# Decoder layer on one core: forming the differences of x ahead of the weight splits, and moving the second pair's raw weights in the queues

## The chip, the cores and the metric

One core of one Trainium2 chip. The metric is the device time of one execution in microseconds; the time before is the median of 3 runs, 643.26 us (642.44 to 646.47).

## The reference

One layer of a post-norm decoder, batch 1, 512 tokens, width 1024, all in float32:

```python
proj = h @ w_in[l]                               # (512, 1024) @ (1024, 4096)
q, k, v, p, g = jnp.split(proj, [512, 1024, 1536, 2048], axis=-1)
y_attn = moba_attention(q.reshape(hs), k.reshape(hs), v.reshape(hs), rel_bias) @ w_branch_attn[l]
y_pool = multiscale_pool(p, w_pool_group[l], pool_scale[l]) @ w_branch_pool[l]
gates = jax.nn.sigmoid(g.astype(jnp.float32)).astype(h.dtype).reshape(B, S, N_BRANCHES, D)
mixed = gates[:, :, 0] * y_attn + gates[:, :, 1] * y_pool
h = layer_norm(ALPHA * h + mixed @ w_out[l], ln1_g[l], ln1_b[l])
a, u = jnp.split(h @ w_ffn_in[l], 2, axis=-1)    # 2 x 2816 columns
a = causal_dwconv(a, conv_w[l], conv_b[l])
f = (jax.nn.gelu(a, approximate=False) * u) @ w_ffn_out[l]
h = layer_norm(ALPHA * h + f, ln2_g[l], ln2_b[l])
```

The attention has 8 heads of 64 with a relative bias by distance; the pool mixer takes trailing means over 2, 4, 8 and 16 tokens for four groups of 128 channels. The change concerns the first tenth of the program, where `x @ w_in` is computed.

## The kernel before, in words

**Split products.** Every float32 matrix product is made of three matmuls (`mm3`). Each operand is split into a high half, a rounded copy that ACT makes, and a low half, the source minus that copy, which DVE makes (`split`, L70 and L71). The three matmuls are high by high, high by low and low by high.

**Chunks of weights.** `chunks` lists all weights in the order of use. `fetch` takes the next one: a DMA on SP's queue into `wraw` (three places), then the split into `whi` and `wlo` (five places, `RING`). `weights(i)` fetches up to three chunks ahead, but not beyond `state["limit"]`. Chunks 0 to 3 are the columns of v, chunk 4 is `p3` and chunk 5 is `p2` (two column tiles of the pool input, computed plainly by `in_tile`), chunks 6 to 9 are pair 0, chunks 10 to 13 pair 1, and so on up to pair 4.

**Pairs.** Two column tiles a and u are computed together by seven half-size products instead of eight (`seven`). Pair 0 holds pool tiles 0 and 1; pairs 1 to 4 hold one tile of q and one of k each. The weights of a pair come as four quarters: A (tile a as it is), X (u's first half twice, to which a's first half and u's second half are added), D (u's second half) and Y (made by DVE from X and A, L185). X needs two DMAs: a plain one on SP (L173), and, when that has landed, an accumulating one on POOL's queue (L175). A pair runs on PE in the order A twice, the Y part left over from the pair before, X, Y, D, X again, and keeps its last Y part for the next pair.

On the side of x, a pair needs four differences of the four blocks of x: nT1, T3, nT2, T4 (`t_form`, L244 and L247 on DVE), each split into halves. They are formed in place, in the two raw tiles `xr[0]` (blocks b11 and b12) and `xr[1]` (b21 and b22): nT1 and T3 replace `xr[0]`, nT2 and T4 replace `xr[1]`. Once they have been split, both tiles serve as places for raw weights (`homes`): X of pair n lies in one half of `xr[0]`, D of pair n in a quarter of `xr[1]`, and the two last quarters of `xr[1]` are working space of the pairs.

**The order around the change.** `load_x` brings x in eight tiles and splits each, with the four chunks of v between them. Then follow in the program: the split of the group weights `wg` (L350), the matmuls of v, during which `weights` fetches chunks 4 to 6 (p3, p2 and A of pair 0), the four differences with their splits (L475 to L478), the bias table `F_sb` (17 small copies, L372), `in_tile` for p3, its pool sum (four additions on DVE, L439), `write_end`, which fills the tile `neg` and writes it as the end of the strip table `F_d` in DRAM (L382 and L383), and `in_tile` for p2. The instructions of an engine are put in order when the program is built, by a planner that works with modelled times; the queues then run in that order. `tc.issue_after(ins)` holds the instructions of a block that lie on the engine of `ins` behind it on that engine, and leaves the other engines alone. `fetch` uses it to keep the plain DMA of pair 1's X behind the write of `neg` on SP:

```python
if (n, f, q) == ("i", 1, "X"):
    held.enter_context(tc.issue_after(state["neg"].ins))
```

`EARLY` and `AHEAD` say how many chunks ahead of its use a raw quarter is asked for. The first table of a strip is written by POOL (`write_table`, L378) behind the last accumulating DMA.

Of the kernel before, what the change touches and what calls it, by code (L numbers as in the profile page):

```python
# [10 lines left out]
AF = mybir.ActivationFunctionType  # L11
# [5 lines left out]
D = 1024  # L17
# [29 lines left out]
def layer_kernel(ctx: ExitStack, tc: tile.TileContext, xT, x, w_v, w_c, rel_bias, invcnt, w_group,  # L47
                 pscale, w_br, w_out, lnr, w_fi, convp, w_fo, out):
    nc = tc.nc
# [9 lines left out]
    def bank(name):  # L59
        return ps.tile([P, S], F32, tag="ps", name=name)  # L60
# [5 lines left out]
    def split(hi, lo, src, copy=None):  # L66
        if copy:
            copy(hi, src)
        else:
            nc.scalar.activation(hi, src, AF.Copy)  # L70
        state["lo"] = nc.vector.tensor_tensor(lo, src, hi.bitcast(F32), op=ALU.subtract)  # L71
        return state["lo"]

# [4 lines left out]
    at = {}  # L78
# [36 lines left out]
    state = {"next": 0, "limit": WO0 - 1}  # L115

    def fetch(pool=None, early=None):
        i = state["next"]
        state["next"] = i + 1
        for q, ahead in AHEAD.items():  # L120
            while coming[q]:
                key = coming[q][0]
                n, f = key
                lead_ = EARLY.get((n, f, q), ahead)
                if not homes.get((n, q)) or at[n, f, q] > i + (lead_ if q != "A" or (n, f - 1) in pair_of else 0):
                    break
                with ExitStack() as held:
                    if (n, f, q) == ("i", 1, "X"):
                        held.enter_context(tc.issue_after(state["neg"].ins))
                    if (n, f, q) in (("i", 1, "D"), ("i", 2, "A"), ("i", 2, "X"), ("i", 2, "D")):  # L130
                        held.enter_context(tc.issue_after(state["plain"].ins))
                    if (n, f, q) == ("i", 2, "X"):
                        held.enter_context(tc.issue_after(state["sum"].ins))
                    fetch_raw(coming[q].pop(0), q)
        if isinstance(chunks[i], tuple):
            ready[i] = (fetch_fo if i >= FO0 else fetch_seven)(i, *chunks[i])
            return
        raw = wp.tile([P, D], F32, tag="wraw", name=f"wraw{i}", bufs=3)
        if pool is None:
            hi = wp.tile([P, D], F32R, tag="whi", name=f"whi{i}", bufs=RING)  # L140
            lo = wp.tile([P, D], F32R, tag="wlo", name=f"wlo{i}", bufs=RING)
        else:
            hi = pool.tile([P, D], F32R, name=f"whi{i}")
            lo = pool.tile([P, D], F32R, name=f"wlo{i}")
        parts = 2 if early else 1
        for c in range(parts):
            sl = slice(c * (D // parts), (c + 1) * (D // parts))
            (nc.scalar if early else nc.sync).dma_start(raw[:, sl], chunks[i][:, sl])
            split(hi[:, sl], lo[:, sl], raw[:, sl], fast if early and c == 0 else None)
            if c == 0 and early:  # L150
                early()
        ready[i] = (hi, lo)
# [8 lines left out]
    homes = {(n, "A"): araw for n in "igf"}  # L161

    def fetch_raw(key, q):
        a, u = pair_of[key]
        r = raws[key, q] = homes[key[0], q](key[1])
        if q == "A":
            nc.sync.dma_start(r, a)
        elif q == "D":
            nc.sync.dma_start(r, u[:, S:])
        else:  # L170
            v = r.rearrange("p (a c) -> p a c", a=2)
            (pst, pn), (est, _) = u.ap
            state["plain"] = nc.sync.dma_start(  # L173
                v, bass.AP(tensor=u.tensor, offset=u.offset, ap=[[pst, pn], [0, 2], [est, S]]))
            state["acc"] = nc.gpsimd.dma_start(  # L175
                v, bass.AP(tensor=a.tensor, offset=a.offset, ap=[[pst, pn], [u.offset + S - a.offset, 2], [est, S]]),
                accum_op=ALU.add)
# [54 lines left out]
    t1, t2 = slice(0, 256), slice(256, 512)  # L232
    k1, k2 = slice(0, 4), slice(4, 8)
    parts = ("nT1", "T3", "nT2", "T4")
# [3 lines left out]
            pending.pop()()  # L238


    def t_form(n, tt, b11, b12, b21, b22):
        if n in ("nT1", "T3"):
            v, a = {"nT1": (b11, b11), "T3": (b12, b22)}[n]
            nc.vector.tensor_tensor(v, a, b12, op=ALU.subtract)  # L244
        else:
            v, a = {"nT2": (b22, b11), "T4": (b21, b22)}[n]
            nc.vector.scalar_tensor_tensor(v, a, -1.0, v, op0=ALU.mult, op1=ALU.subtract)  # L247
        split(*tt[n], v)

    def s_mm(key, q, part, act_, b, start, pin=False):  # L250
        wh, wl = split3(weights(at[(*key, q)]), 4 if q == "D" else KT)
# [48 lines left out]
    wg_raw = av.tile([P, 4, P], F32, tag="strip", name="wg_raw")  # L300
# [5 lines left out]
    ti = {n: tuple(pw.tile([P, 4, 256], F32R, name=f"i{n}_{q}") for q in ("hi", "lo")) for n in parts}  # L306
    pw.tile([P, 48], F32, name="pw_gap2")
    xr = [pw.tile([P, 4, S], F32, name=f"xr{n}") for n in range(2)]
# [38 lines left out]
                            compare_op=ALU.is_equal, fill=0.0)  # L347
    nc.sync.dma_start(wg_raw, w_group)
    wg_hi, wg_lo = (pb.tile([P, 4, P], F32R, name=f"wg_{q}") for q in ("hi", "lo"))
    split(wg_hi, wg_lo, wg_raw)  # L350

    behind.close()
    F_d = dram.tile([H, STRIP], F32, name="F_d")
# [6 lines left out]
    def make_table():  # L360
        F_sb = av.tile([P, S], F32, tag="strip", name="F_sb")
        (pst, pn), _ = rel.ap
        runs, lo_ = _bucket_runs(), 0
        while runs:
            b, n = runs.pop(0)
            step = 0
            if n == 1:
                while runs and runs[0] == [b + n, 1]:
                    step, n = -1, n + 1
                    runs.pop(0)  # L370
            at_ = rel.offset + b - step * (n - 1)
            nc.vector.tensor_copy(F_sb[:H, S - lo_ - n:S - lo_],  # L372
                                  bass.AP(tensor=rel.tensor, offset=at_, ap=[[pst, pn], [step, n]]))
            lo_ += n
        return F_sb
# [4 lines left out]
    def write_end():  # L380
        neg = av.tile([P, S], F32, tag="strip", name="neg")
        nc.vector.memset(neg[:H, :STRIP - S], NEG)  # L382
        state["neg"] = nc.sync.dma_start(F_d[:, S:], neg[:H, :STRIP - S])  # L383

    vv = av.tile([P, NT, H * DH], F32, name="vv", bufs=1)
    bs = [bank(f"v{j}") for j in range(NT)]
    for kt in range(KT):
# [41 lines left out]
    def pool_sum(j, b, sign=1.0, eng=None):  # L429
        eng = eng or nc.gpsimd  # L430
        w = POOL_WINDOWS[j]
        pt = pb.tile([P, PAD + S], F32, tag="tmp", name=f"pt{j}", bufs=TMP)
        nc.gpsimd.memset(pt[:, :PAD], 0.0)
        state["pt"] = nc.scalar.activation(pt[:, PAD:], b, AF.Copy, scale=sign)
        cur, sh = pt, 1
        while sh < w:
            nxt = pb.tile([P, PAD + S], F32, tag="tmp", name=f"pw{j}_{sh}", bufs=TMP)
            o = 2 * sh - 1
            state["sum"] = eng.tensor_tensor(nxt[:, o:], cur[:, o:], cur[:, o - sh:PAD + S - sh], op=ALU.add)  # L439
            cur, sh = nxt, 2 * sh  # L440
        sums[j] = pt, cur
# [22 lines left out]
    def in_tile(kind, j):  # L464
# [6 lines left out]
        else:  # L471
            gslot[j] = gates[:, len(gslot), :]
            nc.vector.tensor_copy(gslot[j], b)

    with tc.issue_after(state["xlo"].ins):  # L475
        t_form(parts[0], ti, xr[0][:, :, t1], xr[0][:, :, t2], xr[1][:, :, t1], xr[1][:, :, t2])
    for n in parts[1:]:
        t_form(n, ti, xr[0][:, :, t1], xr[0][:, :, t2], xr[1][:, :, t1], xr[1][:, :, t2])  # L478
    with tc.issue_after(state["lo"].ins):
        table = make_table()  # L480
    homes["i", "X"] = lambda n: xr[0][:, n % 2 * 2:n % 2 * 2 + 2, :].rearrange("p a c -> p (a c)")
    homes["i", "D"] = lambda n: xr[1][:, n % 2, :]
    raw_q = {}
    raw_k = {}
    state["limit"] = at["i", 0, "A"]
    pool_sum(PLAIN[0], in_tile("p", PLAIN[0]), eng=nc.vector)
    state["limit"] = WO0 - 1
    behind_sum = ExitStack()
    behind_sum.enter_context(tc.issue_after(state["sum"].ins))
    behind_sum.enter_context(tc.issue_after(state["pt"].ins))  # L490
    write_end()
    second = in_tile("p", PLAIN[1])

    def heads_done(p, ba):
# [166 lines left out]
    for f in range(KT - 1):  # L661
# [4 lines left out]
        for br in (1, 0):  # L666
            b = br_mm(f, br)
            if f < GSEVEN:
                t = gslot[8 * br + f]
                nc.vector.tensor_tensor(t, t, b, op=ALU.mult)  # L670
            else:
                t = branch[f, br] = unused.pop(0)
# [199 lines left out]
    def rd(c):  # L872
# [7 lines left out]
    tt = {n: tuple(sp.tile([P, 4, 256], F32R, name=f"{n}_{q}") for q in ("hi", "lo"))  # L880
          for n in ("nT1", "T3", "nT2", "T4")}
# [150 lines left out]
    cut = [bank(f"fo_cut{c}") for c in range(2)]  # L1032
# [23 lines left out]
def _bucket_runs():  # L1056
    b = _bucket_of_dist()
    runs = []
    for v in b:
        if runs and runs[-1][0] == v:  # L1060
            runs[-1][1] += 1
        else:
            runs.append([int(v), 1])
    return runs
# [53 lines left out]
```

## Time and profile before

| | before |
|---|---|
| median of 3 runs | 643.26 us (642.44 to 646.47) |
| the profiled execution | 642.5 us, its span 640.7 us |
| granted TensorE clock | 0.995 |
| PE busy | 627.9 us (98%) |
| DVE busy | 497.3 us (78%) |
| ACT busy | 348.7 us (54%) |
| POOL busy | 117.8 us (18%) |
| DMA | 106.11 MB, mean 166 GB/s |

The span runs from the first to the last instruction; the execution's own time is 1.8 us longer. PE is TensorE, DVE VectorE, ACT ScalarE, POOL GpSimd, SP SyncE, and SPq the DMA queue of SP. A row of the timeline gives the start, the duration, engine, line, operation, output and inputs, how many instructions it merges, and in brackets the idle time before it and what ended it. A row of the waits gives who waited for whom, the total in us, how often, and the longest. The tiles of the pairs of the input stage are called `sai`, `sbi` and `sci` on the output side; `iT` and `inT` are the split differences, `xT` the split x, `araw` the raw A and Y, and `xr` the raw X and D as well as the raw x.

### The profile page before, as it was taken

The numbers are of one execution on the slowest core, as the hardware profiler recorded it, in microseconds if no ns is written. First come the engines' busy times: TensorE is split into PE (matmuls) and PEld (weight loads), VectorE is DVE, ScalarE is ACT, GpSimd is POOL, SyncE is SP. The second block draws the span as 40 slices with busy tenths as digits, with TensorE's granted clock in tenths as the row PEclk, the third lists the DMA queues.
The fourth block names the chain that finished last, engine by engine and source line by source line (L and its number), as shares of the span: only waits on it lengthen the run. The fifth ranks groups of instructions, "written<-read, shape, count | busy, mean of one in ns | idle before, by whom it ended". The sixth has DMA issues, their size and how long they took to land.

```text
span 640.7 us, 10190 instructions
## 1 busy us (share of the span) xinstructions
PE 627.9 (98%) x3910; PEld 560.2 (87%) x3910; DVE 497.3 (78%) x755; ACT 348.7 (54%) x522; POOL 117.8 (18%) x129
## 2 busy tenths in 40 slices
PE   8999999999999999999999999999999999999994
PEld 6888998777788998889999999999998888888884
DVE  6977887786395787399776889888889649798696
ACT  6635777655544557225544566556666336555352
POOL 0032334233132111110010101011002102123202
PEclk9999999999999999999999999999999999999998
DMA  8387746522447515714086686877628955899905
GB/s 326 125 216 190 186 119 209 149 70 95 148 126 209 144 55 177 285 44 165 1 238 156 164 201 158 210 172 202 147 99 283 264 176 123 195 200 196 272 1 131
DMA packets 39312, 106.11 MB, mean 166 GB/s; under 512 B 4304, under 2 KB 4568, under 8 KB 39008
## 3 DMA queue, kind: packets, MB, share of 16 engines
q1 hardware_dynamic: 26576, 71.37, 33.2%
q0 software_dynamic: 12112, 33.05, 26.2%
q10 hardware_dynamic: 576, 1.05, 0.4%
q8 instruction: 30, 0.49, 0.3%
q14 instruction: 18, 0.15, 0.1%
HBM read 100.20 MB, written 3.17 MB: 161 GB/s over the span
## 4 chain that ended last, share of the span: by engine, by line
PE 94%; DMA 3%; DVE 2%; ACT 0%; issue 0%; DVEq 0%; SPq 0%; ACTq 0%
PE fi L226 5%; PE fi L227 5%; PE fi L223 5%; PE saf L223 4%; PE saf L227 4%; PE saf L226 4%; PE v L399 3%; PE g L223 2%; PE br L223 2%; PE g L227 2%; PE g L226 2%; PE br L226 2%; PE wo L223 2%; PE wo L226 2%; PE wo L227 2%; PE br L227 2%
## 5 line engine op out<-in xcount | busy, mean ns | idle before, releaser
L70 ACT ACTIVATE whi<-wraw 128x1024 fp32r<-128x1024 f32 (+1 forms) x58 | 59.6, 1034 | 51.1 <-DMA wraw<-in_w_fo 10.2
L71 DVE TENSOR_TENSOR wlo<-wraw,whi 128x1024 fp32r<-128x1024 f32 (+1 forms) x59 | 72.1, 1229 | 19.5 <-ACT whi L70 19.4
L71 DVE TENSOR_TENSOR wlo<-araw,whi 128x1024 fp32r<-128x1024 f32 x46 | 56.0, 1225 | 11.3 <-ACT whi L70 10.7
L70 ACT ACTIVATE whi<-araw 128x1024 fp32r<-128x1024 f32 x46 | 48.1, 1058 | 20.2 <-PE saf L226 6.1
L226 PE MATMUL fi<-hT_lo,whi 128*128 128x512 f32 (+1 forms) x168 | 56.7, 339 | 0.0
L227 PE MATMUL fi<-hT_hi,wlo 128*128 128x512 f32 (+1 forms) x168 | 56.7, 339 | 0.0
L223 PE MATMUL fi<-hT_hi,whi 128*128 128x512 f32 (+1 forms) x168 | 56.4, 340 | 0.0
L175 POOL DMA_DIRECT2D xraw<-in_w_fi x14 | 16.9, 1210 | 161.5 <-DVE y L858 69.1
L70 ACT ACTIVATE whi<-tw 128x1024 fp32r<-128x1024 f32 (+1 forms) x30 | 29.4, 982 | 20.3 <-PE fi L226 7.5
L71 DVE TENSOR_TENSOR wlo<-tw,whi 128x1024 fp32r<-128x1024 f32 (+1 forms) x30 | 33.3, 1128 | 5.6 <-ACT whi L70 5.5
L227 PEld LDWEIGHTS fi<-hT_hi,wlo 128*128 128x128 f32 x168 | 31.9, 190 | 3.4
L226 PEld LDWEIGHTS fi<-hT_lo,whi 128*128 128x128 f32 x168 | 31.9, 190 | 3.4
L223 PEld LDWEIGHTS fi<-hT_hi,whi 128*128 128x128 f32 x168 | 31.6, 190 | 3.4
L530 POOL TENSOR_SCALAR pp<-pp,rs 128x128 f32<-128x128 f32 (+3 forms) x32 | 26.8, 850 | 37.7 <-DVE rs L527 26.6
L226 PE MATMUL saf<-hT_lo,whi 128*128 128x256 f32 x112 | 31.6, 282 | 0.0
L223 PE MATMUL saf<-hT_hi,whi 128*128 128x256 f32 x112 | 31.6, 282 | 0.0
L227 PE MATMUL saf<-hT_hi,wlo 128*128 128x256 f32 x112 | 31.5, 282 | 0.0
L223 PE MATMUL sbf<-T_hi,whi 128*128 128x256 f32 x112 | 31.3, 280 | 0.0
L223 PE MATMUL saf<-nT_hi,whi 128*128 128x256 f32 x112 | 31.3, 279 | 0.0
L227 PE MATMUL saf<-nT_hi,wlo 128*128 128x256 f32 x112 | 31.3, 279 | 0.0
L227 PE MATMUL sbf<-T_hi,wlo 128*128 128x256 f32 x112 | 31.2, 279 | 0.0
L226 PE MATMUL saf<-nT_lo,whi 128*128 128x256 f32 x112 | 31.2, 279 | 0.0
(346 smaller groups left out, 2105.9 us busy)
## 6 DMA issues: line engine op xcount, KB each, us to landing
tw<-in_w_fo POOLq DMA_DIRECT2D x20, 512.0 KB, 7.7
wraw<-in_w_fi SPq DMA_DIRECT2D x16, 512.0 KB, 3.3
araw<-in_w_fi SPq DMA_DIRECT2D x14, 512.0 KB, 4.3
xraw<-in_w_fi SPq DMA_DIRECT2D x14, 512.0 KB, 4.4
xraw<-in_w_fi POOLq DMA_DIRECT2D x14, 512.0 KB, 7.6
wraw<-in_w_c SPq DMA_DIRECT2D x10, 512.0 KB, 4.2
tw<-in_w_fo SPq DMA_DIRECT2D x10, 512.0 KB, 6.5
wraw<-in_w_fo SPq DMA_DIRECT2D x10, 512.0 KB, 7.3
```

The source lines that it names most:

```text
L70: nc.scalar.activation(hi, src, AF.Copy)
L71: state["lo"] = nc.vector.tensor_tensor(lo, src, hi.bitcast(F32), op=ALU.subtract)
L175: state["acc"] = nc.gpsimd.dma_start(v, bass.AP(tensor=a.tensor, offset=a.offset, ap=[[pst, pn], [u.offset + S - a.offset, 2], [est, S]]), ...
L223: ins = nc.tensor.matmul(out_, wh, ah, start=start, stop=False, **kw)
L226: nc.tensor.matmul(out_, wh, al, start=False, stop=False, **kw)
L227: nc.tensor.matmul(out_, wl, ah, start=False, stop=stop, **kw)
L399: nc.tensor.matmul(bs[j], xs_[j][a], (wh, wl)[b], start=kt == 0 and n == 0, stop=False)
L530: nc.gpsimd.tensor_scalar(pp[:, offs[i]:offs[i] + n], pp[:, offs[i]:offs[i] + n], rs[:, i:i + 1], 1.0, op0=ALU.mult, op1=ALU.mult)
```

## The change

The four differences are separated from their splits (`cut=False`). DVE forms nT1, T3 and nT2 straight after the last split of x, then nT1 and T3 are split; then chunk 4 (p3) is fetched, held behind these splits on ACT and DVE; then T4 is formed, nT2 and T4 are split, and chunks 5 and 6 are fetched behind them, followed by the table, the end of the strip table (`write_end`) and the split of `wg`. The limit of 3 keeps chunks 4 to 6 out of the loop over v. The homes of D are dealt out anew: pairs 0 and 1 share the first quarter of `xr[1]`, then they alternate, where before pair 1 had the second quarter.

```diff
-            nc.scalar.activation(hi, src, AF.Copy)
+            state["hi"] = nc.scalar.activation(hi, src, AF.Copy)
...
-    def t_form(n, tt, b11, b12, b21, b22):
+    def t_form(n, tt, b11, b12, b21, b22, cut=True):
...
-        split(*tt[n], v)
+        if cut:
+            split(*tt[n], v)
+        return v
...
     wg_hi, wg_lo = (pb.tile([P, 4, P], F32R, name=f"wg_{q}") for q in ("hi", "lo"))
-    split(wg_hi, wg_lo, wg_raw)
...
+    state["limit"] = 3
     vv = av.tile([P, NT, H * DH], F32, name="vv", bufs=1)
...
+    blocks = [xr[k][:, :, t] for k in range(2) for t in (t1, t2)]
     with tc.issue_after(state["xlo"].ins):
-        t_form(parts[0], ti, xr[0][:, :, t1], xr[0][:, :, t2], xr[1][:, :, t1], xr[1][:, :, t2])
-    for n in parts[1:]:
-        t_form(n, ti, xr[0][:, :, t1], xr[0][:, :, t2], xr[1][:, :, t1], xr[1][:, :, t2])
-    with tc.issue_after(state["lo"].ins):
+        formed = [t_form(parts[0], ti, *blocks, cut=False)]
+    formed += [t_form(n, ti, *blocks, cut=False) for n in parts[1:3]]
+    for n in range(2):
+        split(*ti[parts[n]], formed[n])
+    state["limit"] = at["i", 0, "A"]
+    with tc.issue_after(state["lo"].ins), tc.issue_after(state["hi"].ins):
+        fetch()
+    formed.append(t_form(parts[3], ti, *blocks, cut=False))
+    for n in range(2, 4):
+        split(*ti[parts[n]], formed[n])
+    with tc.issue_after(state["lo"].ins), tc.issue_after(state["hi"].ins):
+        while state["next"] <= state["limit"]:
+            fetch()
         table = make_table()
+        write_end()
+        split(wg_hi, wg_lo, wg_raw)
     homes["i", "X"] = lambda n: xr[0][:, n % 2 * 2:n % 2 * 2 + 2, :].rearrange("p a c -> p (a c)")
-    homes["i", "D"] = lambda n: xr[1][:, n % 2, :]
+    homes["i", "D"] = lambda n: xr[1][:, (0, 0, 1, 0, 1)[n], :]
...
-    state["limit"] = at["i", 0, "A"]
     pool_sum(PLAIN[0], in_tile("p", PLAIN[0]), eng=nc.vector)
...
-    write_end()
     second = in_tile("p", PLAIN[1])
```

## The prediction

> **What bounds the kernel now.** I read the page's first line, then the waits of PE, then PE's instructions one by one around each wait, then the chain of work that ended last, and only then the queues that feed it.
>
> ```profile
> span 640.7 us, 10190 instructions
> ```
>
> ```profile
> PE warm_ps L318 <- DVE warm L315: 1.2, 1, 1.2
> PE sbi L223 <- ACT whi L70: 1.2, 1, 1.2
> PE sai L223 <- ACT whi L70: 0.4, 1, 0.4
> PE v L399 <- DVE whi L287: 0.4, 1, 0.4
> PE sbi L227 <- DVE wlo L71: 0.3, 1, 0.3
> ```
>
> The program is bound by PE. All its listed waits are five; two belong to the start, and three (1.2, 0.4 and 0.3 us, tiles `sai` and `sbi` of the input pairs) lie between 42 and 54 us. Nothing after that stops PE, so whatever this edit can win lies in that stretch. "Idle" understates it, because a matmul that follows a gap also delays the next one. PE's own rows show it by their starts:
>
> ```profile
> 42.45 0.28 PE L227 MATMUL sbi<-iT_hi,wlo 128*128 128x256 f32 x1
> 42.70 0.38 PE L223 MATMUL sai<-inT_hi,whi 128*128 128x256 f32 x1
> 42.92 0.28 PE L226 MATMUL sai<-inT_lo,whi 128*128 128x256 f32 x1
> 43.65 0.39 PE L223 MATMUL sai<-xT_hi,whi 128*128 128x256 f32 x1 [0.45 <-ACT whi L70]
> 43.87 0.28 PE L226 MATMUL sai<-xT_lo,whi 128*128 128x256 f32 x1
> 43.99 0.28 PE L223 MATMUL sci<-xT_hi,whi 128*128 128x256 f32 x1
> ...
> 50.43 0.28 PE L227 MATMUL sci<-xT_hi,wlo 128*128 128x256 f32 x1
> 51.92 0.38 PE L223 MATMUL sbi<-iT_hi,whi 128*128 128x256 f32 x1 [1.22 <-ACT whi L70]
> ...
> 52.72 0.40 PE L227 MATMUL zb<-difs,wg_lo 128*128 128x512 f32 x1
> 53.42 0.39 PE L227 MATMUL sbi<-iT_hi,wlo 128*128 128x256 f32 x1 [0.30 <-DVE wlo L71]
> ...
> 55.30 0.28 PE L226 MATMUL sci<-xT_lo,whi 128*128 128x256 f32 x1
> 55.49 0.38 PE L227 MATMUL sai<-inT_hi,wlo 128*128 128x256 f32 x1
> ```
>
> A 256-column matmul starts 0.12 us after the one before (43.87 to 43.99), a 512-column one takes about twice that. What the starts show above this pace:
>
> - place 1, the Y quarter of pair 0: 0.25, 0.22, 0.73 and 0.22 instead of 0.12 each, that is 0.13 + 0.10 + 0.61 + 0.10 = 0.94 us; the last of these is the matmul after a gap, and I put the same 0.10 to each of the three gaps below
> - place 2, the X quarter of pair 1: 1.49 instead of 0.12, 1.37 + 0.10 = 1.47 us
> - place 3, the low half of that X: 0.70 instead of about 0.23, 0.47 + 0.10 = 0.57 us
> - place 4, the low half of Y of pair 1: 0.19 instead of 0.12, 0.07 + 0.10 = 0.17 us
>
> Together **3.15 us**. Why place 2 exists is told by the chain, in order of time:
>
> ```profile
> 33.74 0.72 DVE pw L439
> ...
> 36.62 0.18 DVE neg L382
> 36.81 0.29 SPq L383
> 37.16 4.31 DMA xr<-in_w_c
> 41.46 0.30 issue
> 41.76 9.03 DMA xr<-in_w_c
> 50.81 0.70 DVE araw L185
> ```
>
> DVE fills the `neg` tile only after the four additions of the first pool sum; SP's write of it (L383) waits for that; the plain DMA of pair 1's X is queued behind that write (the hold in `fetch`), lands 4.31 us later, and only then can POOL issue the accumulating one, which takes 9.03 us. The splits start at 50.81, when PE has just run dry. D of pair 1 and Y of pair 1 follow from it.
>
> **The change part by part.** No instruction is added or removed: the same four differences, eight half-splits, three weight splits, table, `neg` and `wg` split are issued in another order. So the sum consists of arrivals alone.
>
> ```profile
> 16.56 1.22 DVE L244 TENSOR_TENSOR xr<-xr 128x1024 f32<-128x1024 f32 x1
> 22.84 1.22 DVE L71 TENSOR_TENSOR wlo<-wraw,whi 128x1024 fp32r<-128x1024 f32 x1
> 23.98 1.22 DVE L71 TENSOR_TENSOR iT_lo<-xr,iT_hi 128x1024 fp32r<-128x1024 f32 x1
> 30.32 1.50 DVE L372 COPY F_sb<-rel 8x16 f32<-8x16 f32 x17
> 37.53 1.83 DVE L71 TENSOR_TENSOR wlo<-xr,whi 128x1024 fp32r<-128x1024 f32 x2 [0.74 <-ACT whi L70]
> ```
>
> *Differences first.* 22.84 to 23.98 gives 1.14 us per full-width DVE operation. X of pair 0 goes where nT1 and T3 lie, so it waits for three differences and two splits. Before, the second of these splits (row 23.98) ended at 25.20, with `wg` and two weight splits among them; now five operations from 16.56 end near 16.56 + 5 x 1.14 + 0.1 = 22.3, **2.9 us earlier**.
>
> *Weight splits later.* The split of p3 becomes the sixth operation: low half done near 23.5. PE's X quarter of pair 0 ends with the row at 42.45; its 36 matmuls (A twice, X) at 0.12 begin near 38.3, and the 48 of p3 and p2 at 0.23 before them near 27.3, where p3 is first wanted: 3.8 us of cover. p2 and A of pair 0 end near 28 to 29; PE wants p2 near 32.8 and A near 38.3. If the four copies of `v` on ACT come ahead of p2's high half, p2's low half ends near 28.2 + 1.06 + 1.14 = 30.4, still 2.4 us of cover. Cost nothing; were the cover gone, each us would be one us of PE, but it would come off the 3.15 us above first, as places 1 to 4 wait for arrivals and not for PE.
>
> ```profile
> 25.56 2.64 ACT L395 ACTIVATE vv<-v 128x512 f32<-128x512 f32 x4 [1.54 <-PE v L227]
> ```
>
> *Place 1.* The queues now:
>
> ```profile
> 25.22 0.38 SPq L173 DMA_DIRECT2D xr<-in_w_c  x1
> 29.36 1.37 POOL L175 DMA_DIRECT2D xr<-in_w_c  x1 [27.96 <-DMA xr<-in_w_c]
> 36.43 1.58 ACT L70 ACTIVATE whi<-xr 128x1024 fp32r<-128x1024 f32 x2 [2.80 <-DMA xr<-in_w_c]
> 39.22 1.06 POOL L439 TENSOR_TENSOR pw<-pt 128x527 f32<-128x527 f32 x1 [3.12 <-ACT pt L434]
> ```
>
> X of pair 0 took 4.14 us from SP's issue to POOL's and 7.07 us from there to ACT's split: 22.3 + 11.2 gives 33.5, or 34.0 as A of pair 1 (freed by p3's later split) now shares the transfers. Even behind the four pool additions (they end near 36.4), its low half and D's (1.83 us) are done by 38.3, the two halves of Y (0.7 each) by 39.7, Y's high half at 40.8, its low half at 42.0. PE, at full pace from 38.3 with 36 matmuls of 0.12, wants Y at 42.6. Place 1 goes, with 0.6 us to spare.
>
> *Places 2 to 4.* `neg` is now filled behind the table: 11 operations of 1.14 and the 1.50 us of copies from 16.56 end near 30.6, or up to 33 if ACT's copies of `v` hold the last splits; SP's write and X's plain DMA go at 31 to 33, landing 4.3 us later, at 35.5 to 37.5. On POOL, two things can stand ahead of the accumulating DMA: the clearing of the second pool tile (it waits for DVE's additions, 33.74 plus three of 0.72, about 36) and its first addition (39.22 to 40.28). The trace does not show which order the planner will choose; the ends are 35.5 and 40.3, and I take 36.5, because the plain DMA lands before ACT can hand POOL that addition. The accumulation took 7.07 us for pair 0 and 9.03 for pair 1, so X lands at 43.5 to 45.5 (ends 35.5 + 7.07 = 42.6 and 40.3 + 9.03 = 49.3). PE's place for it moves to 51.92 - 1.37 - 0.94 = 49.6; the high half needs about 1.1 us (1.58 for two of ACT's splits, X and the half as wide D) and the low half 1.2 more, so anything that lands by 47.4 removes places 2, 3 and 4.
>
> The Trainium skill (DMA: Bandwidth & Descriptors, Anatomy of one DMA, software path) gives such a transfer about 2.0 us plus its bytes over 436 kB per us, an estimate of 3.2 us for 512 KB. By it X would land near 40 and the first rival below would be empty; the rows have 7.07 and 9.03, and they decide.
>
> *D in the first quarter's place.* D of pair 1 now waits for D of pair 0 to be split (row 37.53, done by 39.3 before, near 38.4 after). SP stands still until then; behind it are A and X of pair 2, X held in any case by Y's reading of X of pair 0 (39.7 above). Issued at 38.4 and with the 4.14 us of the plain DMA above, D lands near 42.6; PE wants it after X, past 50: 7 us of cover. What is queued behind it has later due times still.
>
> *What is late next.* With PE about 3 us further on, X of pair 2 would be next: its plain DMA waits for Y of pair 0 to read the place, which comes earlier too. Later stages show no PE wait and are supplied through slots that PE frees. I allow 0.4 us for new small waits, the size of the smaller ones listed above (0.3 to 0.45).
>
> Sum: -3.15 + 0.4 = **-2.75 us** (ends -3.2 and, with new waits of 1.2, the largest wait now, -2.0). The profiled execution took 642.5 us for its span of 640.7, so 639.75. The median of the three timed runs, 643.26, stands 0.8 above it, their lowest, 642.44, beside it. Off the median that gives 640.5; the forecast's own range goes from 642.44 - 3.2 = 639.2 to 643.26 - 2.0 = 641.3.
>
> **The rivals.**
>
> *X still late (a gain of about 1.2).* POOL does its addition first and the transfer takes 9.03 again: landing 49.3, high half 50.4, low half 51.6 against 49.6 and 49.8. PE then loses about 2.0 us at places 2 and 3, and 1.2 of 3.2 is won: 642.1. For it: that addition stood ahead of this DMA before. Against: the plain DMA then landed after it; now it should land before.
>
> *Hidden or given back (no gain).* The 3 us return as waits at a later pair or in the heads. For it: the planner's order is fixed at build time, and an order that fits the old arrivals need not fit the new ones. Against: the list of PE's waits has none behind these places. That includes the case that SP's order doesn't change in spite of the edit. 643.3.
>
> *Slower: a queue blocked at its head.* ACT and DVE work in order, and ACT already stood 2.80 us in front of a split whose DMA had not landed (row 36.43). The planner now sees X of pair 1 early; if it puts that split ahead of Y's of pair 0 on ACT, and X really lands at 45, Y's high half comes at 45 + 2.1 = 47.1 while PE wants it at 42.6: 4.5 us lost in place of 3.15, so +1.35, 644.6. It decides from a landing after 41.5 (42.6 less 1.06 for X's split) with that order. Against: Y's weight slot is asked for two chunks ahead of X's, and X's slot is only free when PE is through with A of pair 0, 12 matmuls before 42.6, at 41.1.
>
> The granted clock was 1.00 in the 9.3 us from 50.7 that hold the longest of these waits:
>
> ```profile
> 50.70:60.00 9.30, 7.78 (x60) 7.18 (x60) 8.10 (x11) 6.72 (x11) 1.25 (x2) 1.00 0.70 196
> ```
>
> The Trainium skill (TensorE: Matmul & The Clock Gate, Part 1) says that about 3.4 us without work halves PE's clock until as long a busy stretch has passed. No gap here is that long; a wait of 4.5 us would be, and by an estimate from that page the last rival would cost half of 3.4 us more, 646.3.
>
> **How the numbers follow.** Forecast 0.68, X still late 0.12, given back 0.07, slower 0.13. The forecast's 640.5 is the time. The range takes in the first two rivals, the spread between the timed runs (0.8 us), and the nearer part of the third: 639.0 to 644.0. Left out are the farther part of the slower case (0.09) and about 0.05 on the fast side and beyond. One per cent is 6.4 us, about what a measurement of this kernel can tell from no change. All the PE loss in reach is 3.2 us, so faster by more has 0.01; slower by more than 6.4 us needs the blocked queue to cost over 9 us, 0.04 out of that case; 0.95 within.
>
> **What would show it.** Right: SP's `neg` write near 31 to 33 and X of pair 1 right behind; X of pair 0 on SP near 22.3; POOL's second accumulating DMA near 36.5, ahead of the addition of the second pool sum; PE's waits on `sai` and `sbi` gone, with the `sbi` matmuls of pair 1's X near 49.6; the first `p` matmul still near 27.4. Wrong: a PE wait at 27.4 or 32.8 (weight splits too late), an accumulating DMA at or after 40, an ACT split of `xr` that waits for a DMA ahead of Y's, or new PE waits of over 1 us after 56.

## The result, and the profile after

| | before | after |
|---|---|---|
| median | 644.07 us (641.53 to 646.47, 8 runs) | 639.94 us (638.85 to 643.1, 8 runs) |
| profiled execution, its span | 642.5 us, 640.7 us | 639.83 us, 638.1 us |
| granted TensorE clock | 0.995 | 0.995 |

The ratio of the times is 0.9943, with a 95% interval of 0.9917 to 0.9968: the kernel became faster by 4.1 us (2.1 to 5.3), 0.6%, which lies under the one per cent that the prediction takes for what a measurement can tell; the interval excludes no change all the same. The forecast was 640.5 us.

First the page's span and the whole list of PE's waits, as they were shown of before:

```profile
span 638.1 us, 10194 instructions
```

```profile
PE warm_ps L320 <- DVE warm L317: 1.2, 1, 1.2
PE tr L597 <- DVE nm L531: 0.8, 1, 0.8
PE v L401 <- DVE whi L289: 0.3, 1, 0.3
```

The waits on `sai` and `sbi` are gone. By the starts of the matmuls, read as in the prediction, nothing above the pace is lost between 16 and 80 us, where before had 3.18 us. In their place stands one wait of 0.8 at a transpose `tr`, at 100.85 us (the rows of after, then of before):

```profile
99.00 1.03 PE L597 MATMUL tr<-ident,pp 128*128 128x128 f32 x8
100.85 0.41 PE L597 MATMUL tr<-ident,pp 128*128 128x128 f32 x2 [0.81 <-DVE nm L531]
101.23 0.50 PE L223 MATMUL g<-xT_hi,whi 128*128 128x512 f32 x1
```

```profile
102.33 1.56 PE L585 MATMUL tr<-ident,pp 128*128 128x128 f32 x10
103.88 0.50 PE L223 MATMUL g<-xT_hi,whi 128*128 128x512 f32 x1
```

The wait takes back a part of the gain: the first of these transposes starts 3.33 us earlier than before, the `g` matmul behind them 2.65 earlier, so 0.7 us go there. The rest of the account is small: the start is 0.3 us worse (the first `p` matmul at 27.73 instead of 27.40), and two gaps at 90.4, 0.4 us in all, were in the kernel before alone. The stages behind the first tenth all begin 2.6 to 2.7 us earlier: the first `br` matmul at 164.9 (167.6 before), the first `foe` matmul at 523.8 (526.4). That is the difference of the two spans, 2.6 us.

The timeline of SP's queue, then of POOL, where the prediction had its first numbers:

```profile
22.41 0.38 SPq L173 DMA_DIRECT2D xr<-in_w_c  x1
...
32.10 0.29 SPq L384 DMA_DIRECT2D F_d<-neg  x1
32.44 0.38 SPq L173 DMA_DIRECT2D xr<-in_w_c  x1
...
38.75 0.33 SPq L169 DMA_DIRECT2D xr<-in_w_c  x1
39.35 0.61 SPq L173 DMA_DIRECT2D xr<-in_w_c  x1
40.01 0.54 SPq L169 DMA_DIRECT2D xr<-in_w_c  x1
```

```profile
36.92 1.23 POOL L175 DMA_DIRECT2D xr<-in_w_c  x1 [7.61 <-DMA xr<-in_w_c]
...
40.05 1.06 POOL L441 TENSOR_TENSOR pw<-pt 128x527 f32<-128x527 f32 x1 [1.20 <-issue]
```

X of pair 0 goes out at 22.41 (25.22 before), `neg` at 32.10 (36.81), X of pair 1 right behind at 32.44 (37.16). POOL issues the accumulating DMA at 36.92 (41.76) and only then does the first addition of the second pool sum. D of pair 1 follows at 38.75, X and D of pair 2 at 39.35 and 40.01 (40.90 and 41.39 before). What came of it on ACT and on PE:

```profile
34.16 1.06 ACT L70 ACTIVATE whi<-xr 128x1024 fp32r<-128x1024 f32 x1 [0.19 <-DMA xr<-in_w_c]
...
42.89 1.06 ACT L70 ACTIVATE whi<-xr 128x1024 fp32r<-128x1024 f32 x1
```

```profile
44.81 0.28 PE L223 MATMUL sbi<-iT_hi,whi 128*128 128x256 f32 x1
44.93 0.28 PE L226 MATMUL sbi<-iT_lo,whi 128*128 128x256 f32 x1
```

The row at 42.89 is the high half of pair 1's X. It has no bracket: the data lay there when ACT came to it. It took at most 42.89 - 36.92 = 5.97 us from POOL's issue, where before took 9.03. And PE reads it sooner than was thought: the planner moved the first two matmuls of this X forward, to 44.81, so the split, done at 43.95, is 0.86 us ahead of its use.

### The profile page after: what moved, and what is told of

The parts are those of the page before. It is cut to its first block, busy times and chain, and to the rows that moved or that the text cites. A ratio compares the mean times of both kernels' runs of the same rounds, so it can differ in the third digit from the quotient of the medians.

```text
span 638.1 us, 10194 instructions
## 1 busy us (share of the span) xinstructions
PE 626.8 (98%) x3910; PEld 560.6 (88%) x3910; DVE 499.0 (78%) x755; ACT 348.7 (55%) x522; POOL 116.6 (18%) x129
## 4 chain that ended last, share of the span: by engine, by line
PE 97%; DVE 1%; ACT 1%; issue 0%; DMA 0%; DVEq 0%
PE fi L227 5%; PE fi L226 5%; PE fi L223 5%; PE saf L223 4%; PE saf L227 4%; PE saf L226 4%; PE v L401 3%; PE br L223 2%; PE br L226 2%; PE wo L223 2%; PE br L227 2%; PE wo L226 2%; PE wo L227 2%; PE g L223 2%; PE g L226 2%; PE g L227 2%
## 5 line engine op out<-in xcount | busy, mean ns | idle before, releaser
L71 DVE TENSOR_TENSOR wlo<-araw,whi 128x1024 fp32r<-128x1024 f32 x46 | 55.8, 1220 | 11.0 <-ACT whi L70 10.3
L223 PE MATMUL sbf<-T_hi,whi 128*128 128x256 f32 x112 | 31.4, 280 | 0.0
L226 PE MATMUL sbf<-T_lo,whi 128*128 128x256 f32 x112 | 31.2, 279 | 0.0
```

The lines of the kernel that those rows point to most:

```text
L223: ins = nc.tensor.matmul(out_, wh, ah, start=start, stop=False, **kw)
L226: nc.tensor.matmul(out_, wh, al, start=False, stop=False, **kw)
```

## What made the accumulating DMA shorter

This was not in the prediction, and it decides most of what follows. The view of the DMA queues gives for a stretch of time each queue's packets, megabytes and the share of the 16 engines' time; q1 is SP's queue, q0 is POOL's. The kernel before, four stretches of 2 us from 40 us on (POOL issues at 41.76):

```profile
q1 hardware_dynamic: 318, 0.79, 102.7%
q1 hardware_dynamic: 244, 0.52, 94.9%
q1 hardware_dynamic: 195, 0.34, 51.5%
q0 software_dynamic: 72, 0.15, 45.3%
q0 software_dynamic: 196, 0.36, 98.7%
```

The first three rows are q1 in 40 to 42, 42 to 44 and 44 to 46, the last two q0 in 44 to 46 and 46 to 48. The kernel after, stretches from 38 us on (POOL issues at 36.92):

```profile
q0 software_dynamic: 55, 0.11, 62.3%
q0 software_dynamic: 201, 0.40, 107.5%
q1 hardware_dynamic: 3, 0.01, 0.8%
q1 hardware_dynamic: 321, 0.62, 94.3%
q0 software_dynamic: 48, 0.03, 9.1%
```

Here q0 in 38 to 40 and 40 to 42, q1 in 40 to 42, and both in 42 to 44. Before, the accumulating DMA moved nothing until 44.5, while SP's queue moved X and D of pair 2 among others, and it shared the engines after that. After, it is the one that is through first, and SP's, issued at 39.35 and 40.01, move 0.01 MB until 42. Before, X of pair 2 was issued 0.86 us ahead of the accumulating DMA of pair 1's X; after, it is 2.43 us behind it.

Stretches of half a us show where the time went. The first packets of POOL's DMA lie in 44.5 to 45.0 before, some 3 us behind the issue, and in 38.5 to 39.0 after, some 2 us behind it, although SP's queue moved nothing from 38.0 to 38.5. So about 2 us pass without anything ahead of it, and waiting for its turn is only about one of the three us won. The others pass behind the first packet: before, SP's queue moves 0.51 MB from 44.5 to 48.5 beside it; after, 0.01 MB from 38.5 to 42. A plain DMA of SP starts sooner: X of pair 3, issued at 47.71 in the kernel after, has its first packets in 48.5 to 49.0. So, by an estimate from these two rows, an issue by POOL that leads by less than about a us is not ahead at the engines.

The profiled executions in which X of pair 1 goes out alone behind `neg`, sorted by that lead of POOL's issue over X of pair 2 (the experiments are told below; the last column is an upper bound where ACT came late, and the kernel with p3 last is not in it, as ACT comes to the split 8.3 us after the issue there without having waited; by the view of the DMAs its X landed 5.6 us after the issue, with a lead of 4.83):

| execution | POOL's issue | ahead of X of pair 2 by | from issue to ACT's split |
|---|---|---|---|
| e2_neg_late | 41.43 | -2.82 us | 9.7 us |
| before_look2 | 43.86 | -2.75 | 9.4 |
| before | 41.76 | -0.86 | 9.05 |
| before_look1 | 41.16 | -0.59 | 8.9 |
| e1_look | 39.29 | +0.48 | 10.3 |
| e1_neg_early | 39.87 | +0.90 | 8.0 |
| e7_neg_early_d_first | 37.44 | +1.97 | 5.4 |
| e4_d_second | 37.65 | +2.01 | 5.65 |
| after_look | 36.63 | +2.08 | 5.6 |
| after | 36.92 | +2.43 | 5.97 |

Two groups: 5.4 to 6.0 us from a lead of 2 us on, 8.0 to 10.3 us below 1 us. So an issue that comes a little sooner wins three or four us at the end, if it gets ahead of the next plain transfers by enough. A lead of 0.48 or 0.90 us was not enough (with 0.90, POOL's first packets lie in 41.5 to 42.0, SP's in 42.0 to 42.5), so the order of issue alone isn't the rule. That the order at the engines decides is read from these ten rows and the queues' rows. The experiment with D of pair 1 below, which changes the order on SP alone, agrees with it; the one made to force the order (the last one) did not force it.

## The experiments

In the short diffs the lines are those of the program as given in the section on the change.

**One half of the change at a time.** The write of `neg` alone: the kernel before, with the end of the strip table behind the bias table.

```diff
         table = make_table()
+        write_end()
...
-    write_end()
     second = in_tile("p", PLAIN[1])
```

> The kernel before with one line moved: the end of the strip table is filled and written right behind the table instead of behind the first pool sum; the differences of x keep their old place. Arrival theory (the one of the prediction): X of pair 1 leaves SP near 32 instead of 37.2, POOL's accumulating transfer goes near 36, X lands at 43 to 45 and PE's losses at places 2, 3 and 4 (1.47 + 0.57 + 0.17 = 2.2 us) vanish, while place 1 (0.94 us, the wait on sai at 43.65) stays: span 640.7 - 2.2 = 638.5. Rival, the order of the differences is what pays: X of pair 0 is as late as before, nothing changes, 640.7.

Measured: 643.68 us median (641.01 to 648.09, 12 runs), ratio 1.0005 (0.9979 to 1.0031); the profiled execution 645.81, with a start 1.7 us longer than before's (the first `p` matmul at 29.11). The theory of the arrivals, by which this half alone should bring most of the gain, failed. Its chain of work that ended last, and PE at the end of it:

```profile
34.04 5.53 DMA xr<-in_w_c
39.57 0.30 issue
39.87 7.92 DMA xr<-in_w_c
...
47.87 1.07 ACT whi L70
```

```profile
46.05 0.28 PE L227 MATMUL sai<-inT_hi,wlo 128*128 128x256 f32 x1
48.98 0.39 PE L223 MATMUL sbi<-iT_hi,whi 128*128 128x256 f32 x1 [2.65 <-ACT whi L70]
```

X landed at 47.8 instead of 50.8, three us sooner, but PE now asks for it at 46.3, where before asked at 50.7: the planner, which sees X earlier, also put its first matmuls earlier. The wait grew from 1.22 to 2.65 us. And a price came on top. The windows (stretch, length, busy time of PE, of its weight load, DVE, ACT and POOL with counts, granted clock, DMA share, GB/s):

```profile
47.00:50.50 3.50, 1.52 (x12) 1.52 (x13) 1.54 (x2) 2.12 (x4) 2.57 (x3) 1.00 0.79 266
50.50:53.90 3.40, 3.40 (x18) 3.40 (x17) 2.42 (x5) 1.01 (x2) 0.11 (x1) 0.51 1.01 195
53.90:57.00 3.10, 3.10 (x27) 3.10 (x27) 1.79 (x3) 1.84 (x2) 0.56 (x1) 0.99 0.58 203
```

The granted clock stands at 0.5 for 3.4 us from 50.55 on, 1.6 us after PE went on; a 256-column matmul starts every 0.21 us there instead of every 0.12. By these two paces that loses about 1.5 us. The Trainium skill (TensorE: Matmul & The Clock Gate, Part 1) names 3.4 us as the window in which idleness is judged; the length of the slow stretch agrees with it, but the 2.65 us of this wait are less than a whole window.

The differences alone: the kernel after, with the write of `neg` back behind the pool sum.

```diff
         table = make_table()
-        write_end()
         split(wg_hi, wg_lo, wg_raw)
...
+    write_end()
     second = in_tile("p", PLAIN[1])
```

> The changed kernel with the end of the strip table put back behind the first pool sum; the differences stay ahead of the weight splits. Arrival theory: place 1 is gone (0.94 us), but X of pair 1 leaves SP near 37 again and lands near 50 by the clock, whatever PE has won before; PE reaches its place 0.94 us earlier and waits 0.94 us longer there. So the gain is lost again and the span is 640.7, give or take 0.4, with a wait on sbi of some 2.1 us. Rival, the two parts add up: span 640.7 - 0.94 = 639.8, with the old wait of 1.2 us on sbi.

Measured: 644.49 us (641.27 to 645.82, 12 runs), ratio 1.0003 (0.9982 to 1.0024). The direction was right, the size was not. POOL does its addition first and issues at 41.43, and PE waits 2.90 us:

```profile
39.24 1.06 POOL L441 TENSOR_TENSOR pw<-pt 128x527 f32<-128x527 f32 x1 [3.62 <-ACT pt L436]
41.43 1.23 POOL L175 DMA_DIRECT2D xr<-in_w_c  x1 [1.12 <-DMA xr<-in_w_c]
```

```profile
52.28 0.38 PE L223 MATMUL sbi<-iT_hi,whi 128*128 128x256 f32 x1 [2.90 <-ACT whi L70]
```

```profile
52.75:56.00 3.25, 3.25 (x14) 2.71 (x13) 3.25 (x6) 2.74 (x5) 0.00 (x0) 0.50 0.33 98
56.25:58.00 1.75, 1.75 (x17) 1.75 (x17) 1.68 (x3) 0.38 (x1) 0.00 (x0) 1.00 0.94 341
```

The half clock again, for 3.4 us (52.7 to 56.1). X of pair 0 was split as early as in the kernel after, so PE comes to X of pair 1 sooner and waits longer for it: the gain of place 1 turns into a longer wait at place 2, plus the clock. So neither half alone brings anything that can be measured, and both together bring 0.6%.

**The hold of X behind the write of `neg`.** X of pair 1 held behind the last load of x instead, first in the kernel before, then in the kernel after:

```diff
-                        held.enter_context(tc.issue_after(state["neg"].ins))
+                        held.enter_context(tc.issue_after(state["x"].ins))
```

> The kernel before with X of pair 1 held on SP behind the last load of x instead of behind the end of the strip table; nothing else. Arrival theory: the end of the table was only in the way; X of pair 1 follows X of pair 0 on SP near 25.6, lands well before 49 and places 2 to 4 (2.2 us) vanish. The transfers of both X then run side by side, so X of pair 0 lands 0 to 1.5 us later than 36.4 and place 1 grows by as much: span 638.5 to 640. Rival, the hold protects X of pair 0: place 1 grows by more than 2.2 us and the span is 640.7 or more.

> The changed kernel with X of pair 1 held on SP behind the last load of x instead of behind the end of the strip table. All other engines keep their order; on SP X of pair 1 goes right behind X of pair 0, near 22.8 instead of 32.4. Theory, crowded transfers: X of pair 1 lands long before PE asks for it, which wins nothing, since PE has no wait here; X of pair 0 lands 2 to 2.5 us later (34.2 to about 36.6, as between the kernel before and e3_no_hold, 36.43 to 38.85), which the four pool additions on DVE (until 36.9) nearly hide, so Y of pair 0 is 0 to 0.6 us late: span 638.1 to 638.8. Rival, the hold is as needed here as in the kernel before: a wait on sai of 2 us or more, span 640 or more.

Measured: in the kernel before 643.82 us (12 runs), ratio 0.9994 (0.9973 to 1.0014); in the kernel after 640.23 us (12 runs), ratio 0.9952 (0.9931 to 0.9973), which is the time of the kernel after. In the kernel before the rival was right: both X go out together and share the transfers, so X of pair 0 lands late.

```profile
24.81 0.89 SPq L173 DMA_DIRECT2D xr<-in_w_c  x2
```

```profile
38.85 1.58 ACT L70 ACTIVATE whi<-xr 128x1024 fp32r<-128x1024 f32 x2 [5.13 <-DMA xr<-in_w_c]
```

```profile
45.13 0.39 PE L223 MATMUL sai<-inT_hi,whi 128*128 128x256 f32 x1 [2.32 <-ACT whi L70]
46.08 0.39 PE L223 MATMUL sai<-xT_hi,whi 128*128 128x256 f32 x1 [0.45 <-ACT whi L70]
```

Its split begins at 38.85 instead of 36.43, and the loss moves from places 2 to 4 to place 1, 3.29 us in all against 3.18. The hold buys pair 0 its speed, so to take it away is no way to the gain. In the kernel after the same edit delays X of pair 0 as well (split at 36.06 instead of 34.16), but there the cover is large enough, and PE loses nothing between 16 and 80 us.

**D of pair 1.** The quarter dealt as before, in the kernel after:

```diff
-    homes["i", "D"] = lambda n: xr[1][:, (0, 0, 1, 0, 1)[n], :]
+    homes["i", "D"] = lambda n: xr[1][:, n % 2, :]
```

> The changed kernel with D of pair 1 in the second quarter again, as before the change; the other engines keep the order of the changed kernel, on SP D of pair 1 now goes right behind X of pair 1, ahead of A of pair 2. Arrival theory: D's 256 KB run beside the accumulating transfer of X, which lands up to 1 us later than 42.9; its high half has 0.86 us before PE uses it, so PE loses 0 to 0.3 us: span 638.1 to 638.5. Rival, the quarter is a needed part of the change: X lands more than 1.5 us later, a wait on sbi near 45 of 1 us or more, span 639.1 or more.

Measured: 640.22 us (639.25 to 641.73, 11 runs), ratio 0.9949 (0.9929 to 0.9969), its span 637.8, 0.3 us below the range expected, with a start 0.6 us shorter (the first `p` matmul at 27.10). D of pair 1 now goes out right behind X, at 32.24, POOL issues 0.7 us later (37.65), and PE loses 0.34 us. In the full change the quarter brings nothing that can be measured. In the kernel of the first experiment it is different: the quarter of D given to it in addition, with the order on PE, DVE, ACT and POOL unchanged and only D of pair 1 and A of pair 2 changing places on SP.

```diff
-    homes["i", "D"] = lambda n: xr[1][:, n % 2, :]
+    homes["i", "D"] = lambda n: xr[1][:, (0, 0, 1, 0, 1)[n], :]
```

> The kernel of e1_neg_early (end of the strip table early, differences in their old place) with the changed kernel's places of D: D of pair 1 in the first quarter. All engines keep e1's order; on SP D of pair 1 goes behind A of pair 2. Theory, crowded transfers: in e1 the plain transfer of X took 5.53 us beside D and A, and the accumulating one 7.9 us beside X and D of pair 2. Without D of pair 1 beside it the plain one takes about 4.4, POOL's starts about 1 us earlier, runs longer before pair 2's transfers begin, and X lands some 2 us earlier against PE; the wait of 2.65 us on sbi falls to about 0.5, PE's granted clock no longer drops to 0.5 behind it: span 638.1 to 638.8. Rival, the differences have to come first as well: X still lands after PE asks for it by 1.5 us or more, span 639.5 to 642.

Measured: 641.5 us (639.55 to 647.51, 12 runs), ratio 0.9985 (0.9956 to 1.0014). The profiled execution took 640.74 us and has no wait at X of pair 1:

```profile
37.44 1.23 POOL L175 DMA_DIRECT2D xr<-in_w_c  x1 [1.57 <-DMA xr<-in_w_c]
```

POOL issues at 37.44 instead of 39.29 in the second profile of the first experiment (below), whose `neg` write went out at the same time (31.70, here 31.76); it gets 1.97 us ahead of X of pair 2, and the transfer takes 5.4 us. PE loses 1.42 us between 16 and 80, and no clock is lost. But 3 of the 12 timed runs took over 645 us, with granted clocks of 0.990 to 0.994, and by the medians the kernel is not told from before, nor from the first experiment. In this profile the quarter removes the crowd around X of pair 1; the three long runs suggest that it does not always do so.

**p3's split between the others.** The fetch of p3 moved behind the last difference's splits, in the kernel after:

```diff
-    with tc.issue_after(state["lo"].ins), tc.issue_after(state["hi"].ins):
-        fetch()
     formed.append(t_form(parts[3], ti, *blocks, cut=False))
```

> The changed kernel with chunk 4 (p3) fetched behind all four differences and their splits instead of behind the first two. It tries the cover of the weight splits: p3's low half was done at 23.5 and PE asks for p3 near 27.5. Theory, arrivals: the low half now comes behind T4, two more splits and a part of the table's copies, near 27.5 to 28.5, and the high half near 26.5; PE loses 0 to 1 us at the first p matmuls, not more; X of pair 0 is not touched: span 638.1 to 639.1. Rival, the weights have ample cover and the place of p3 is without effect on PE: 638.1, with no wait at p.

Measured: 640.28 us (639.71 to 642.59, 10 runs), ratio 0.996 (0.994 to 0.9981), the span 638.9. The size lies in the range expected, the place doesn't. There is no wait at `p`: the planner put the first matmuls of pair 0's A among those of p3, at 28.64 instead of 33.62. Instead place 1 is partly back:

```profile
43.90 0.39 PE L223 MATMUL sai<-xT_hi,whi 128*128 128x256 f32 x1 [0.44 <-ACT whi L70]
```

That is 0.8 us above the pace, the largest difference found in this profile between it and the kernel after, whose spans differ by 0.8.

**How much the executions differ.** Four more single profiles, on one chip: the kernel before twice, the kernel after, and the first experiment again.

> The kernel before, unchanged, for another look. Its timed runs reach from 640 to 646.5 us, those of the changed kernel from 638.9 to 643.1. Theory, the wait for X of pair 1 varies: in some executions it is longer than 2.5 us and PE's granted clock falls to 0.5 behind it, as in e1_neg_early and e2_neg_late, for 1.6 us more; then a look at a slow execution shows it: span 642 to 644 with a wait of 2.5 us or more on sbi. Rival, the spread lies in the start alone: the wait on sbi is 1.2 us as before and the span differs by what PE loses ahead of 16 us.

> The kernel before once more, with the same expectations as for the first look: either a wait on sbi of 2.5 us or more with a granted clock of 0.5 behind it, or a wait of 1.2 us and a span that differs by the loss at the start.

> The changed kernel, unchanged, for another look. Theory and rival agree that PE loses nothing between 16 and 60 us; theory, arrivals: X of pair 1 lands 0.5 us or more ahead of PE in this execution too, and the span differs from 638.1 by the loss at the start alone (1.9 us in the first profile, of which 0.3 more than in the kernel before).

> The kernel of e1_neg_early, unchanged, for another look: its profile had a slow start, PE lost about 1.5 us more ahead of 16 us than in the kernel before. Theory, crowded transfers: with an ordinary start the wait on sbi is still 2 to 3 us, since arrivals and PE shift together; the span is 642 to 642.6 if the clock drops behind it and 640.4 to 641 if not. Rival, the slow start made the wait: with an ordinary start it is under 1 us and the span is 638.5 to 639.5.

Measured: before 642.84 and 645.94, after 639.01, the first experiment 649.68 us. The waits of PE in the second of these profiles of before, and the windows around the one at X of pair 1:

```profile
PE sbi L223 <- ACT whi L70: 2.6, 1, 2.6
```

```profile
51.25:54.25 3.00, 0.57 (x5) 0.36 (x4) 0.93 (x2) 0.97 (x2) 0.00 (x0) 1.00 0.98 172
54.25:58.00 3.75, 3.61 (x14) 3.21 (x15) 3.75 (x6) 3.36 (x6) 0.00 (x0) 0.55 0.28 84
```

So the kernel before has executions in which the start alone loses 3.57 us (0.94 in the first of the two), `neg` goes out at 38.79 instead of 36.14, X of pair 1 is that much later, PE waits 2.6 us for it, and the half clock follows: 4.36 us lost between 16 and 80 us, against 3.04 in the first and 3.18 in the profile of the prediction. The kernel after lost nothing there in either of its two profiles, with 1.94 and 1.01 us at the start. In the first experiment's second profile it is worse still, a wait of 5.88 us:

```profile
44.80:46.40 1.60, 0.00 (x0) 0.00 (x0) 0.36 (x2) 0.00 (x0) 1.06 (x1) 1.00 1.09 255
46.40:50.60 4.20, 0.00 (x0) 0.00 (x0) 0.00 (x0) 1.05 (x2) 2.21 (x2) 0.51 0.96 246
50.60:56.60 6.00, 5.94 (x28) 5.95 (x29) 4.05 (x6) 2.08 (x6) 0.41 (x2) 0.50 0.52 138
```

The clock falls 1.7 us after PE ran dry and stays down for 10.2 us, 6 of them in work: 9.29 us are lost in all.

How often this happens can be read from the granted clocks of the timed runs, as one stretch of 3.4 us at half clock takes 0.003 off the mean: 0.993 in the second profile of before, 0.995 and 0.996 in the two without it. Of the 29 runs of the kernel before that were timed together with the kernel with p3 last, 14 show 0.992 or 0.993 and took 644.5 to 646.4 us; 15 show 0.995 to 0.997 and took 640.2 to 643.6. Of the 34 timed together with the first two experiments, 11 show 0.993 or less. The 8 runs of the kernel after, and the 33 of its variants with p3 last, without the hold and with D in the second quarter, all show 0.995 or more and took 638.7 to 643.1. By this sign the kernel before falls into the half clock in a third to a half of its runs, and the kernel after in none of these.

**An order forced, which was not.** The kernel before, with the place of X dealt so that X of pair 2 has to wait until pair 1 is through with its own:

```diff
-    homes["i", "X"] = lambda n: xr[0][:, n % 2 * 2:n % 2 * 2 + 2, :].rearrange("p a c -> p (a c)")
+    homes["i", "X"] = lambda n: xr[0][:, (0, 1, 1, 0, 1)[n] * 2:(0, 1, 1, 0, 1)[n] * 2 + 2, :].rearrange("p a c -> p (a c)")
```

> The kernel before, with X of pair 2 put into the place of X of pair 1, so that its plain DMA (and D of pair 2 behind it on SP) can't be issued until pair 1 is done with that place. The question is what makes the accumulating DMA of pair 1's X slow. Theory, order of arrival: it takes 8.9 to 9.4 us in the kernel before because the plain DMAs of X and D of pair 2 are issued 0.6 to 2.8 us ahead of it and go first; without them its time from POOL's issue to ACT's split falls to 5.4 to 6.5 us, and the wait of PE at that X (0.7 to 2.6 us before) goes. Rival, the transfer is as slow whatever lies beside it, as POOL, DVE or the accumulation itself set its pace: 8.9 us or more again, and the wait of PE stays. The total says little: X of pair 2 now comes late, and PE is expected to lose 2 to 8 us there, 643 to 650 us.

Measured: 658.65 us. It doesn't answer its question. A plain DMA of an X still goes out at 41.06, which by the order must be pair 3's, whose place is free, 3 us ahead of POOL's issue at 44.05; the split comes at 53.29, 9.24 us later, and PE waits 2.63 us, much as in the second of the two profiles of before above. D of pair 2 was gone from the crowd and that changed nothing. As the DMA of X of pair 2 stands ahead of Y of pair 1 in the program, Y of pair 1 is made from pair 2's X here; it waits for that, and PE for it, 7.48 us, hence the time. Whether X would come in 6 us with nothing ahead of it in the kernel before has not been tried.

## Why the prediction was right

The time came out 0.6 us from the forecast, by the mechanism named: the 3.15 us at places 1 to 4 went, and 0.7 came back at one new wait. Step by step:

- *Differences first* and *place 1*: X of pair 0 on SP at 22.41, said 22.3; its split at 34.16, said 33.5 to 34.0. Place 1 is gone. The low half of Y was done at 43.15, said 42.0, and PE used it from 43.63: 0.5 us to spare, said 0.6.
- *Weight splits later*, costed at nothing: the low half of p3 was done at 23.5, as said, that of p2 at 31.4, a microsecond after the latest time given; PE came to p2 at 33.17 (said 32.8) and to its low half at 34.10. The cover held. The kernel with p3 last says where it would have gone: to place 1, not to `p`.
- *Places 2 to 4*: `neg` at 32.10, POOL's issue at 36.92, ahead of the addition: said 31 to 33 and 36.5. The next two numbers were wrong in opposite ways. X was to land at 43.5 to 45.5 and was there by 42.89, because 7.07 to 9.03 us had been taken for the accumulating DMA and it took at most 5.97. And PE was to ask for it at 49.6 and asked at 44.81, because the prediction kept PE's order and only shifted it. With the term of 7.07 to 9.03 and the true demand, X's high half would have been ready at 45.1 to 47.0, after PE's 44.81: the forecast holds because both errors fell together, and that they did was luck. The `sbi` matmuls at 49.6 are the one sign in the list of signs that did not show.
- *D in the first quarter's place*, costed at nothing, with 7 us of cover: true of the full change (0.9949 without it, 0.9943 with it), but the prediction looked only at when D lands, not at what D's absence from the queue does for X. In the first experiment's kernel it is worth 1.85 us of POOL's issue, by which the transfer gets ahead of X of pair 2, and the wait at `sbi` is gone in the profile.
- *What is late next*: 0.4 us had been allowed for new small waits. One came, at `tr` and not at an X: 0.7 us by the starts, less the 0.4 that before lost at 90.4. The start was 0.3 us worse, which differs from one execution to another anyway (0.94 to 3.57 us over the profiles of before and after).
- *The rivals.* X still late is what the second experiment shows; it was priced at a loss of 2.0 us and costs 2.9 and the clock. Given back is not what happened: the list of waits has one new one, worth 0.7 of the 3 us. The blocked queue did not occur: ACT did not stand in front of X at 42.89.
- The term for the clock, left at half of 3.4 us in the slower rival alone, was bound to a wait of 4.5 us. Waits of 2.57 to 2.90 us were enough. The Trainium skill's page on the clock speaks of a whole idle window of 3.4 us (TensorE: Matmul & The Clock Gate, Part 1); these three waits are shorter, and the measurement decides.

By the two profiles the gain is 2.7 us, by the medians 4.1; the interval, 2.1 to 5.3, holds both. The prediction worked from a profile of before without the half clock, and its sum of 2.75 is a sum for such executions: the 15 runs of before at 0.995 or more have a median of 642.5, from which 639.94 is 2.6 us away, though the two were not timed together. The larger gain of the medians fits the longer wait with the half clock, into which a third to a half of the runs of before fall and none of after; the prediction had no term for it on this side.

## What to carry to other kernels

A transfer's duration is not its own: when two queues feed the same DMA engines, ask which is issued first, and by how much, before taking its duration from a row. When a planner orders the work, an earlier arrival also moves the use forward, so compare arrival and demand in the new order, not in the old one shifted. And two halves of an edit that each change nothing can still be the gain together, if the one only moves the wait to where the other removes it.

## What the runs showed of the hardware

After the start, the granted clock fell to 0.50 in five executions, after waits of 2.57, 2.63, 2.65, 2.90, 5.88 and 7.48 us, and not after waits of 0.45, 1.22 and 2.32 us. It fell 0.2 to 1.6 us after the end of the four shorter waits, and 1.7 and 3.8 us after the beginning of the two long ones. It stayed for 3.4 us behind the shorter waits and for 10.2 behind the long ones, one or three times the same length. So a wait of 2.6 us cost 4.3 us here, and to shorten it below that is worth more than its own length.

In the first experiment both queues moved little from 41 to 44 us though three transfers were issued (q0 0.02 MB in 40 to 42 and 0.08 MB in 42 to 44, q1 0.15 and 0.07 MB), and then shared the engines evenly. What held them is not shown by any run.
